# The first MLP's gate computed beside its up product, and the rest of layer 0's conditioning in steps of 512 columns

## The chip, the core and the metric

The kernel runs on one core of one Trainium2 chip. A core has TensorE (PE; its weight loads are listed apart as PEld), VectorE (DVE), ScalarE (ACT), GpSimd (POOL) and SyncE (SP, which here issues most transfers), each with a queue of its own that it works through in order; they meet only at semaphores. The metric is the device time of one execution in microseconds.

## The reference, cut to what matters

The program is one inference step of a two-layer trunk for a prompt of 1024 tokens and a sample of 32 tokens, so 1056 token columns in all. Every layer is conditioned: from a vector `c` (one for the prompt, one for the sample) six vectors of 1024 values come out of one matrix, and scale, shift and gate the two sublayers.

```python
def ada_mod(c, w, b):
    return jax.nn.silu(c) @ w + b
...
for l in range(DEPTH):
    sh1, sc1, g1, sh2, sc2, g2 = jnp.split(ada_mod(c, p['w_ada'][l], p['b_ada'][l])[:, None, :], 6, axis=-1)
    u = x * (1 + sc1) + sh1
    if l < N_A_LAYERS:
        y, cv, C, n, m = mlstm_mixer(u, ...)
    else:
        ... # attention on one shared K/V, itself conditioned by w_ada_kv
    x = layer_norm(ALPHA * x + (1 + g1) * y, p['ln_g'][l, 0], p['ln_b'][l, 0])
    u = x * (1 + sc2) + sh2
    f = jnp.square(jax.nn.relu(u @ p['w_up'][l])) @ p['w_down'][l]
    x = layer_norm(ALPHA * x + (1 + g2) * f, p['ln_g'][l, 1], p['ln_b'][l, 1])
```

All is in 32-bit floats. `g2` of layer 0, the first MLP's gate, is the one that the change moves. `g1`, `sh2` and `sc2` of layer 0 are what else is computed beside the mLSTM; `sh1` and `sc1` come before it.

## The kernel before

**Matmuls.** Activations lie with features on the partitions and tokens along the row. To keep 32-bit accuracy at the fast matmul rate, `split` writes a high half of a tile (a cast on ScalarE, L89) and the remainder (a subtraction on VectorE, L90); `proj` (L118 to L120) then multiplies high by high, high by low and low by high. Weights come in blocks of 512 rows by 256 columns through a ring of three `raw` buffers and are split into a ring of six `wc` buffers.

**Stages of layer 0.** The start loads and transposes the input. The mLSTM projects `v`, `q`, `k` and the output gate `o` head by head and runs the matrix memory chunk by chunk between those matmuls. The output projection (`op_a`) and the first norm follow. Then the MLP, `mlp7`: some blocks of the up projection are computed plainly (`up_tile`), the others in the class `Seven` by seven products instead of eight per 2 x 2 block, whose weight forms (`rdn_u` to `s_u` to `wf_u`) VectorE and ScalarE make one job ahead. Activations are squared, split (`HL`, one buffer) and stored to memory (`hpl`). The down projection of layer 0 (`dn_plain`) goes over eight groups of 512 rows: per group eight feature chunks by token blocks (264 columns in the first group, else 384 or 288), twelve matmuls a tile, and an eviction on VectorE that multiplies by the gate and adds to `ACX` (L1045). The tile takes one of the eight PSUM banks until then. In group 0, four weight blocks `w_dn_0_0` to `w_dn_0_3` serve four tiles by two chunks each, that is eight tiles each.

**Conditioning.** A product of a vector with a matrix is done on VectorE: `cs` holds silu(c) with one value per partition, and a multiply-add takes a slice of the matrix (128 rows by some columns), multiplies by that value and adds to an accumulator, for each of the two vectors and eight slices of 128 rows. `ada_cols` (L238, L241) does this in steps of 256 columns (two chunks of 128), `ada_wide` (L274, L276) in steps of 512 with the next load under way. A transpose (L245, L283) and a sum (L246, L285) put partial sums into `cx`, and every eight chunks `ada_sums` finishes with four small matmuls (`adas`, L296) and an addition into `ada`.

**Order.** Python generators are woven by `Flow`. A generator yields how long it wants to wait; every unit of matmul work calls `flow.tick(us)`, which counts the waits down and runs a generator one step when its wait is used up. `flow.finish(gen)` runs a generator to its end at once. A scheduler then sets the static order of each engine's queue with the order of emission as priority; within `Seven`, TensorE's order is that of emission. Three generators carry the conditioning: `ada_l0` beside the mLSTM (32 chunks for layer 0 from column 2048, in a `wc` buffer of its own called `ada_room`, waits `ADA_C`), `ada_some` in `Seven` (8 chunks for the shared K/V, waits `ADA_B = (4.0, 2.0, 1.0, 8.0)`, accumulator `aacc` and loads `rada` in the `raw` ring), and `ada_rest` in the down projection (56 chunks, accumulator `aw`, loads `radw`). The tick of a product of `Seven` is `QN / L.pace`, that is 264 / 480 = 0.55 in layer 0, and there are 154 products. Between the two MLP halves stands:

```python
def seven():
    norms["ada"] = flow.add(ada_some())

def down():
    flow.finish(norms["ada"])
    norms["ada"] = flow.add(ada_rest(), carry=True)
```

## Time and profile before

| | us |
|---|---|
| median of 3 runs | 2436.86 |
| lowest and highest | 2434.49, 2437.28 |
| the profiled execution | 2437.59 |
| its span | 2435.8 |
| VectorE busy in the span | 1987.5 |
| ScalarE busy | 1178.8 |
| first and last conditioning multiply-add beside the mLSTM, start | 70.7, 447.6 |
| the same in `Seven` (`aacc`) | 640.3, 776.7 |
| the same in the down projection (`aw`) | 869.8, 1165.5 |

A row of the profile names a line of the program, an engine, an operation, and what it writes and reads (buffer numbers left out). A wait row says who waited, for whom, the total, how often and the longest. In a time-ordered list a row has its start, the time from the first start to the last end of what it merges, how many (`x8`), and in brackets the idle time ahead of it with what ended it. Durations of instructions in a row overlap at their ends, so the spacing is a little under the duration. Tables of stretches give the busy time of each engine between two points of the span.

### The profile page before, as it was taken

How to read it: one execution, taken by the hardware profiler on the slowest of the kernel's cores; microseconds unless marked ns; L12 is line 12 of the kernel's file. 1: busy time of each engine (PE TensorE's matmuls, PEld its weight loads, DVE VectorE, ACT ScalarE, POOL GpSimd, SP SyncE). 2: the span in 40 equal slices, each digit the busy share in tenths (PEclk: the TensorE clock that was granted, in tenths of full speed). 3: DMA queues.
4: the chain of work that ended last, by engine and by line, in shares of the span. 5: the costliest groups of instructions: out<-in, count | busy, mean ns of one | idle time of the engine just before them, and what ended most of it. 6: DMA issues, size and time to landing. Idle time of an engine off the chain costs nothing.

```text
span 2435.8 us, 44452 instructions
## 1 busy us (share of the span) xinstructions
PE 2363.6 (97%) x17180; PEld 2265.8 (93%) x17180; DVE 1987.5 (82%) x4222; ACT 1178.8 (48%) x2394; POOL 166.6 (7%) x315
## 2 busy tenths in 40 slices
PE   7999999999999999999999999999999999899997
PEld 4999999999999999999989977889999999899997
DVE  4899898788788789999697666755998888887778
ACT  4644456278566620010157566763776777222212
POOL 0211100000000000000001134420000000000003
PEclk9999999999999999999999999999999999999999
DMA  8433223436556897656423220051486779966642
GB/s 297 128 103 98 82 86 102 158 113 215 182 186 194 296 343 266 234 203 232 143 64 97 74 64 1 11 133 36 162 279 233 252 255 341 367 242 232 229 151 72
DMA packets 292151, 423.61 MB, mean 174 GB/s; under 512 B 15576, under 2 KB 221804, under 8 KB 286820
## 3 DMA queue, kind: packets, MB, share of 16 engines
q1 hardware_dynamic: 287908, 390.50, 48.3%
q10 hardware_dynamic: 4032, 30.28, 3.1%
q8 instruction: 135, 2.21, 0.4%
q14 instruction: 76, 0.62, 0.1%
HBM read 304.91 MB, written 118.17 MB: 174 GB/s over the span
## 4 chain that ended last, share of the span: by engine, by line
PE 47%; DVE 12%; DMA 5%; ACT 4%; issue 2%; POOL 1%; SPq 0%; DVEq 0%; ACTq 0%; POOLq 0%
PE dn L1415 11%; PE up L1280 9%; PE dn L120 5%; PE dn L119 5%; PE dn L118 5%; PE pv L1853 3%; PE s L1796 2%; PE pt L1831 2%; DMA rdn_u<-in_w_up_dram 1%; DVE wf_u L90 1%; PE op_b L118 1%; PE op_b L119 1%; PE op_b L120 1%; DVE HL L90 1%; DMA radw<-in_w_ada_dram 1%
## 5 line engine op out<-in xcount | busy, mean ns | idle before, releaser
L1045 DVE SCALAR_TENSOR_TENSOR ACX<-dn,ada,ACX 128x264 f32<-128x264 f32 (+6 forms) x664 | 281.9, 448 | 86.4 <-PE dn L1415 41.4
L1415 PE MATMUL dn<-fx,wf_d 128*128 128x264 f32 x2016 | 254.0, 285 | 6.5 <-DVE ACX L1045 3.5
L1415 PEld LDWEIGHTS dn<-fx,wf_d 128*128 128x128 f32 x2016 | 248.7, 188 | 8.7 <-issue 2.5
L89 ACT CAST w_dn<-raw_dn 128x1024 fp32r<-128x1024 f32 x36 | 37.7, 1050 | 284.1 <-DVE aw L274 172.8
L118 PE MATMUL dn<-hs,w_dn 128*128 128x384 f32 (+2 forms) x512 | 161.3, 316 | 0.8 <-DVE ACX L1045 0.7
L119 PE MATMUL dn<-hs,w_dn 128*128 128x384 f32 (+2 forms) x512 | 160.9, 315 | 0.0
L120 PE MATMUL dn<-hs,w_dn 128*128 128x384 f32 (+2 forms) x512 | 155.9, 314 | 1.8 <-DVE w_dn L90 1.8
L1280 PE MATMUL up<-TF,wf_u 128*128 128x264 f32 x1056 | 143.6, 285 | 1.8 <-ACT H L1283 1.8
L1280 PE MATMUL up<-u,wf_u 128*128 128x264 f32 x1056 | 139.7, 285 | 1.7 <-DVE H L1286 0.8
L1280 PE MATMUL up<-U,wf_u 128*128 128x264 f32 x1056 | 139.6, 285 | 1.6 <-DVE H L1286 1.0
L274 DVE SCALAR_TENSOR_TENSOR aw<-radw,cs,aw 128x512 f32<-128x512 f32 x196 | 139.5, 745 | 0.0
L1280 PEld LDWEIGHTS up<-TF,wf_u 128*128 128x128 f32 x1056 | 134.3, 188 | 3.1 <-ACT H L1283 3.0
L1280 PEld LDWEIGHTS up<-U,wf_u 128*128 128x128 f32 x1056 | 133.1, 188 | 2.7 <-DVE H L1286 1.9
L1280 PEld LDWEIGHTS up<-u,wf_u 128*128 128x128 f32 x1056 | 132.6, 188 | 2.7 <-ACT wf_u L89 0.8
L119 PE MATMUL dn<-U,w_dn 128*128 128x384 f32 (+2 forms) x416 | 129.8, 313 | 0.0
L118 PE MATMUL dn<-U,w_dn 128*128 128x384 f32 (+2 forms) x416 | 129.3, 311 | 0.0
L120 PE MATMUL dn<-U,w_dn 128*128 128x384 f32 (+2 forms) x416 | 125.6, 312 | 0.9 <-DVE w_dn L90 0.9
L238 DVE SCALAR_TENSOR_TENSOR ada_room<-ada_room,cs 128x256 f32<-128x256 f32 x224 | 98.9, 476 | 4.2 <-DMA ada_room<-in_w_ada_dram 4.2
L120 PEld LDWEIGHTS dn<-hs,w_dn 128*128 128x128 f32 x512 | 95.8, 188 | 2.9 <-DVE w_dn L90 2.6
L118 PEld LDWEIGHTS dn<-hs,w_dn 128*128 128x128 f32 x512 | 96.4, 188 | 1.5 <-DVE ACX L1045 1.0
L119 PEld LDWEIGHTS dn<-hs,w_dn 128*128 128x128 f32 x512 | 96.5, 188 | 0.0
L1806 DVE CUSTOM_DVE_ANT_0 p<-s,bias 128x576 f32<-128x576 f32 (+9 forms) x132 | 79.1, 606 | 20.3 <-PE s L1796 13.4
(394 smaller groups left out, 7171.5 us busy)
## 6 DMA issues: line engine op xcount, KB each, us to landing
hpl<-HL SPq DMA_DIRECT2D x144, 264.0 KB
rdn_u<-in_w_up_dram SPq DMA_DIRECT2D x64, 512.0 KB
hd<-HL SPq DMA_DIRECT2D x28, 1056.0 KB
fx<-hd SPq DMA_DIRECT2D x50, 528.0 KB
radw<-in_w_ada_dram SPq DMA_DIRECT2D x24, 1024.0 KB
hd<-HM SPq DMA_DIRECT2D x28, 792.0 KB
raw_up<-in_w_up_dram SPq DMA_DIRECT2D x40, 512.0 KB
raw_dn<-in_w_down_dram SPq DMA_DIRECT2D x36, 512.0 KB
```

The costliest lines, as they stand in the source:

```text
L90: (eng or nc.vector).tensor_sub(dst_l, src, dst_h.bitcast(F32))
L118: nc.tensor.matmul(ps, wh, mov(0, k), start=(k == 0), stop=False)
L119: nc.tensor.matmul(ps, wh, mov(1, k), start=False, stop=False)
L120: nc.tensor.matmul(ps, wl, mov(0, k), start=False, stop=(k == nk - 1))
L238: nc.vector.scalar_tensor_tensor(acc[:, cnd], raw[:, k], sc, acc[:, cnd], op0=ALU.mult, op1=ALU.add)
L274: nc.vector.scalar_tensor_tensor(acc[cnd], raw[:, k], sc, acc[cnd], op0=ALU.mult, op1=ALU.add)
L1045: nc.vector.scalar_tensor_tensor(xs, ps[:, off + o:off + o + mm_], gate[:, fc, cnd:cnd + 1], xs, op0=ALU.mult, op1=ALU.add)
L1280: nc.tensor.matmul(p, self.ws[w][:, wl, k], moving(f, tp, xl, k), start=first and k + n_ == 0, stop=k == 3 and n_ == 2, skip_group_check=n ...
L1415: nc.tensor.matmul(p, ws[w][:, wl, k], t[:, s0, xl], start=first and k + n_ == 0, stop=k == kg - 1 and n_ == 2, skip_group_check=not first)
L1796: nc.tensor.matmul(s[:, b, :w], qst, kk[i][:, g, k0 + j0:k0 + j0 + w], start=(i == 0), stop=(i == 1))
L1806: nc.vector.tensor_tensor_reduce(out=z.rearrange("p (b w) -> p b w", b=np_), in0=s[:, :np_, :w], in1=bt.rearrange("p (b w) -> p b w", b=np ...
L1853: nc.tensor.matmul(pv[64 * e:64 * e + 64, :nq], V[:kp, vt0 + j, g * 64:(g + 1) * 64], pts[e][:kp, j, :nq], start=(j == 0), stop=(j == nt - 1))
```

## The change

The generator beside the mLSTM drops the eight chunks of the first MLP's gate (part 5 of layer 0, from column 5 x 1024) and does the other 24 by `ada_wide` in steps of 512 columns. Its loads are of 1 MB, into the first 2048 columns of `ada_room`, which the two transposes use afterwards; there is no second room, so a new argument `ahead=False` loads a step's matrix when the step begins, waits 3.0, does half the work, waits 2.0 and does the rest. The accumulators are a tile of the `raw` ring, `ada_acc`, held from the first step to the last. The eight chunks go to the head of `ada_some`, in steps of 256 columns as its own, with a finish of the gate (`ada_fix`) between the two sets of eight.

```diff
-    def ada_wide(src, c0, base, nch, mk, tmp_f, raw_f, step):
+    def ada_wide(src, c0, base, nch, mk, tmp_f, raw_f, step, ahead=True):
...
-        load(0)
-        yield step[0]
+        if ahead:
+            load(0)
+            yield step[0]
         for i, (j, half) in enumerate(jobs):
-            load(i + 1)
+            load(i + ahead)
+            if not ahead:
+                yield step[1]
...
-                if k % 2:
+                if k % 2 and (ahead or k == 1):
                     yield step[k // 2]
...
-    ADA_C = (2.0, 0.0, 2.0)
+    ADA_C = (2.0, 3.0, 2.0)
...
     def ada_l0():
         room = ring.tile([P, 2112], F32, tag="wc", name="ada_room", bufs=6)
 
+        acc = raw_tile([P, 2, 512], "ada_acc")
+
         def raw_f(shape, name):
-            return room[:, 1024:2048].rearrange("p (k c) -> p k c", k=4)
+            return room[:, :2048].rearrange("p (k c) -> p k c", k=4)
 
         def tmp_f(shape, name):
-            return room[:, 512:1024] if len(shape) == 2 else room[:, :512].rearrange("p (k c) -> p k c", k=2)
-        yield from ada_cols(a["w_ada"][0], 2048, 16, 32, adat, tmp_f, ADA_C, raw_f)
-        ada_fix(0, [(2, "g"), (4, "sc"), (5, "g")])
+            i = int(name[-1])
+            return room[:, 512 * i:512 * i + 512] if name.startswith("awt") else acc[:, i]
+        yield from ada_wide(a["w_ada"][0], 2048, 16, 24, adat, tmp_f, raw_f, ADA_C, False)
+        ada_fix(0, [(2, "g"), (4, "sc")])
...
     def ada_some():
+        yield from ada_cols(a["w_ada"][0], 5 * D, 40, 8, mm, tmp_t, ADA_B)
+        ada_fix(0, [(5, "g")])
         yield from ada_cols(a["w_ada_kv"], 0, 96, 8, mm, tmp_t, ADA_B)
```

**VectorE's queue at the start of the down projection.** `H` and `HL` are the last activations of the up projection, `ACX` the evictions of the first `dn` tiles, `aw` the conditioning of `ada_rest`, `w_dn` the remainder halves of down weights. Before:

```order
L90 TENSOR_TENSOR HL_15_1_10324<-H_15_1_10098,HL_15_1_10324 128x4x264
L1286 TENSOR_TENSOR H_13_1_10232<-up_13_1_2_10331,H_13_1_10232 128x264
L1045 SCALAR_TENSOR_TENSOR ACX_0_10118<-dn_0_0_0_10408,ada,ACX_0_10118 128x264
L1045 SCALAR_TENSOR_TENSOR ACX_0_10118<-dn_0_0_264_10424,ada,ACX_0_10118 128x264
L276 TENSOR_SCALAR aw_0_0_10469<-radw_0_0_10422,cs 128x512
L276 TENSOR_SCALAR aw_0_1_10470<-radw_0_0_10422,cs 128x512
L1045 SCALAR_TENSOR_TENSOR ACX_0_10118<-dn_0_0_528_10438,ada,ACX_0_10118 128x264
L274 SCALAR_TENSOR_TENSOR aw_0_0_10469<-radw_0_0_10422,cs,aw_0_0_10469 128x512
L274 SCALAR_TENSOR_TENSOR aw_0_1_10470<-radw_0_0_10422,cs,aw_0_1_10470 128x512
L1045 SCALAR_TENSOR_TENSOR ACX_0_10118<-dn_0_0_792_10452,ada,ACX_0_10118 128x232
```

Now (`aacc` is the accumulator of `ada_some`, `aat` its transpose):

```order
L90 TENSOR_TENSOR HL_15_1_10158<-H_15_1_9918,HL_15_1_10158 128x4x264
L1292 TENSOR_TENSOR H_13_1_10066<-up_13_1_2_10165,H_13_1_10066 128x264
L1051 SCALAR_TENSOR_TENSOR ACX_0_9942<-dn_0_0_0_10317,ada,ACX_0_9942 128x264
L90 TENSOR_TENSOR w_dn_0_1_10181<-raw_dn_0_1_10179,w_dn_0_1_10181 128x1024
L238 SCALAR_TENSOR_TENSOR aacc_2_10058<-rada_2_1_10246,cs,aacc_2_10058 128x256 x8
L1051 SCALAR_TENSOR_TENSOR ACX_0_9942<-dn_0_0_264_10333,ada,ACX_0_9942 128x264
L90 TENSOR_TENSOR HL_13_1_10230<-H_13_1_10066,HL_13_1_10230 128x4x264
L245 STREAM_TRANSPOSE aat_2_10256<-aacc_2_10058 128x512
L241 TENSOR_SCALAR aacc_4_10259<-rada_4_0_10260,cs 128x256
L246 TENSOR_REDUCE cx<-aat_2_10256 128x16
L241 TENSOR_SCALAR aacc_4_10259<-rada_4_0_10260,cs 128x256
L238 SCALAR_TENSOR_TENSOR aacc_4_10259<-rada_4_0_10260,cs,aacc_4_10259 128x256 x6
```

Before, four evictions stand among the first four `aw` operations. Now the rest of `ada_some` stands there: 36 multiply-adds, 4 scalings, 3 transposes and 3 sums follow the first eviction, with the second, third and fourth eviction at wide gaps among them. The remainder half of the third weight block, `w_dn_0_2`, comes after the eviction of the thirteenth tile before, and of the sixteenth now, each time ahead of the seventeenth, its first user.

**SP's queue at the same place.** `raw_dn` are down weights on their way in, `radw` the loads of `ada_rest`, `hpl` the stores of activations. Before:

```order
L96 DMA raw_dn_0_0_10274<-in_w_down_dram 128x4x256
L96 DMA raw_dn_0_1_10345<-in_w_down_dram 128x4x256
L1147 DMA hpl_6125<-HL_12_1_10206 256x1x264 x4
L96 DMA raw_dn_0_2_10663<-in_w_down_dram 128x4x256
L96 DMA raw_dn_0_3_10802<-in_w_down_dram 128x4x256
L1624 DMA ACX_1_10406<-xsp_80 128x2112
L261 DMA radw_0_0_10422<-in_w_ada_dram 128x4x512
L1147 DMA hpl_6125<-HL_15_1_10324 256x1x264 x4
L261 DMA radw_0_1_10467<-in_w_ada_dram 128x4x512
L1624 DMA ACX_1_10406<-xsp_80 128x2112
L1147 DMA hpl_6125<-HL_13_1_10392 256x1x264 x4
L261 DMA radw_4_0_10567<-in_w_ada_dram 128x4x512
```

Now (`rada` are the loads of `ada_some`):

```order
L231 DMA rada_2_1_10246<-in_w_ada_kv_dram 128x4x256
L1153 DMA hpl_5931<-HL_15_1_10158 256x1x264 x4
L231 DMA rada_4_0_10260<-in_w_ada_kv_dram 128x4x256
L231 DMA rada_4_1_10270<-in_w_ada_kv_dram 128x4x256
L231 DMA rada_6_0_10284<-in_w_ada_kv_dram 128x4x256
L1153 DMA hpl_5931<-HL_13_1_10230 256x1x264 x4
L261 DMA radw_0_0_10331<-in_w_ada_dram 128x4x512
L231 DMA rada_6_1_10294<-in_w_ada_kv_dram 128x4x256
L261 DMA radw_0_1_10376<-in_w_ada_dram 128x4x512
L1632 DMA ACX_1_10315<-xsp_80 128x2112
L261 DMA radw_4_0_10476<-in_w_ada_dram 128x4x512
L96 DMA raw_dn_0_2_10572<-in_w_down_dram 128x4x256
```

Five of the sixteen loads of `ada_some` now stand between the down weights and the stores, a sixth just ahead of the first `raw_dn`, and the third and fourth down weights have moved behind them and behind three loads of `ada_rest`.

**TensorE's queue, eleventh tile of the down projection.** Before, the tile's matmuls follow each other:

```order
L118 MATMUL dn_0_2_528_10573<-U,w_dn_0_1_10347 128x264
L119 MATMUL dn_0_2_528_10573<-U,w_dn_0_1_10347 128x264
L120 MATMUL dn_0_2_528_10573<-U,w_dn_0_1_10347 128x264
L118 MATMUL dn_0_2_792_10587<-U,w_dn_0_1_10347 128x264
L119 MATMUL dn_0_2_792_10587<-U,w_dn_0_1_10347 128x264
L120 MATMUL dn_0_2_792_10587<-U,w_dn_0_1_10347 128x264
```

Now the four small matmuls that end the second set of `ada_some` stand in it:

```order
L120 MATMUL dn_0_2_528_10482<-U,w_dn_0_1_10181 128x264
L118 MATMUL dn_0_2_792_10496<-U,w_dn_0_1_10181 128x264
L119 MATMUL dn_0_2_792_10496<-U,w_dn_0_1_10181 128x264
L299 MATMUL adas_6_10307<-cx,sel 32x16 x4
L120 MATMUL dn_0_2_792_10496<-U,w_dn_0_1_10181 128x264
L118 MATMUL dn_0_2_792_10496<-U,w_dn_0_1_10181 128x264
L118 MATMUL dn_0_1_792_10430<-U,w_dn_0_0_10110 128x264
```

They read `cx`, so everything behind them in TensorE's queue waits for the last sum on VectorE. The eighth tile (`dn_0_1_792`) is also put behind the ones of the next chunk.

## The prediction

> **What bounds the kernel.** I read the page first (busy time and the chain that ended last), then the table of stretches, then the waits of TensorE, then the tiles of the conditioning work, and last the time-ordered list around the place where layer 0 turns from its up to its down projection.
>
> ```profile
> PE 2363.6 (97%) x17180; PEld 2265.8 (93%) x17180; DVE 1987.5 (82%) x4222; ACT 1178.8 (48%) x2394; POOL 166.6 (7%) x315
> ```
>
> TensorE is busy 97% of the span, so time moves only where TensorE starts or stops waiting. The table of stretches has, behind each stretch's length, the busy time (and instructions) of PE, PEld, DVE, ACT and POOL, then granted clock, DMA share and GB/s:
>
> ```profile
> 61.00:122.00 61.00, 58.67 (x373) 57.30 (x372) 53.57 (x96) 36.97 (x78) 12.69 (x20) 0.97 0.43 128
> 120.00:426.00 306.00, 303.52 (x2017) 286.07 (x2016) 281.56 (x858) 162.66 (x439) 29.18 (x94) 1.00 0.31 94
> 606.00:806.00 200.00, 197.21 (x1606) 195.66 (x1606) 157.55 (x276) 121.31 (x214) 0.00 (x0) 1.00 0.62 197
> 740.00:760.00 20.00, 19.09 (x155) 18.71 (x155) 18.94 (x37) 13.58 (x24) 0.00 (x0) 1.00 0.59 186
> 806.00:862.00 56.00, 54.92 (x453) 54.18 (x452) 43.90 (x72) 40.00 (x70) 0.00 (x0) 1.00 0.89 295
> 868.00:890.00 22.00, 22.00 (x183) 22.00 (x182) 21.34 (x41) 3.08 (x3) 0.00 (x0) 1.00 1.04 383
> 862.00:1160.00 298.00, 296.53 (x1957) 292.77 (x1956) 283.49 (x509) 30.04 (x30) 0.00 (x0) 1.00 0.70 255
> ```
>
> The mLSTM (about 61 to 426) leaves TensorE idle 2.3 + 2.5 us in all, though VectorE is 92% busy. The seven-product up projection (606 to 862) leaves 3.9 us. The down projection (from 862) is the tight one: VectorE 95% busy beside a TensorE that hardly waits, with the DMA engines full at its start. So what leaves the mLSTM leaves a place where it cost little, and what arrives at 806 to 890 arrives where there is least room.
>
> **What the mLSTM loses.** Conditioning there before (count, then min/median/max ns), and, in the time-ordered list, such instructions when they stand in a row:
>
> ```profile
> L238 DVE SCALAR_TENSOR_TENSOR ada_room<-ada_room,cs x224: 451/476/696, 70.7 to 447.6; 128x256 f32<-128x256 f32 x112
> L241 DVE TENSOR_SCALAR ada_room<-ada_room,cs x32: 308/345/355, 70.1 to 437.6; 128x256 f32<-128x256 f32 x32
> L245 DVE STREAM_TRANSPOSE ada_room<-ada_room x16: 679/700/712, 83.3 to 449.2; 128x512 f32<-128x512 f32 x16
> ```
> ```profile
> 773.93 3.25 DVE L238 SCALAR_TENSOR_TENSOR aacc<-rada,cs,aacc 128x256 f32<-128x256 f32 x8
> 868.56 0.88 DVE L276 TENSOR_SCALAR aw<-radw,cs 128x512 f32<-128x512 f32 x2 [1.59 <-DMA radw<-in_w_ada_dram]
> 886.53 1.29 DVE L283 STREAM_TRANSPOSE awt<-aw 128x512 f32<-128x512 f32 x2
> 924.68 2.74 DVE L274 SCALAR_TENSOR_TENSOR aw<-radw,cs,aw 128x512 f32<-128x512 f32 x4
> ```
>
> Eight multiply-adds of 256 columns take 3.25 us, so one costs 0.40; four of 512 take 2.74, so 0.67. Before: 224 x 0.40 + 32 x 0.31 + 16 transposes and 16 sums at 0.64 = 120 us. After: six groups of 512 columns, 84 x 0.67 + 12 x 0.42 + 12 x 2 x 0.64 = 77 us. VectorE is relieved of about 43 us. TensorE can get back only what it waits:
>
> ```profile
> PE ae_ps L567 <- ACT stk L560: 2.2, 1, 2.2
> PE cu L678 <- DVE hn L704: 2.0, 5, 0.9
> ```
>
> The second wait is VectorE's lateness; the first is the gate rows' chain, which VectorE also feeds. I take **-2 us**. Bounds: -4.8 (all idle time of both stretches) to +5.3. The latter is for the new accumulator, which holds one of three raw buffers through the stage, and for the 1 MB loads that wait in SP's queue ahead of weights: one weight load that comes a whole landing late, 5.32 us by the load quoted next. I stay near the first end because the weights' loads stand tiles ahead of use. The conditioning's last sums come earlier, so the first output gate isn't late.
>
> ```profile
> 729.18 5.32 DMA rdn_u<-in_w_up_dram
> ```
>
> **What the up projection gains.** `ada_some` now has eight jobs of two chunks, not four. A product ticks 264/480 = 0.55. The waits 4, 2, 4, 2, 1 then take 8, 4, 8, 4, 2 = 26 ticks a job, and 15 instead of 2 where a set of eight chunks ends. The first set ends at tick 118, as before. 22 jobs of weights x 7 products give 154 ticks, so the second set is only 36 ticks in when the stage ends: one job and the first four operations of the next are done there, and the rest is drained at once by the call at the start of the down projection.
>
> In the 36 products (36 x 12 matmuls x 0.12 us = 52 us, so 811 to 862) VectorE gets 20 x 0.40 + 4 x 0.31 + 1.3 = 10.5 us, where it had 12.1 us idle. The nearest row is 740:760, where such work ran before: VectorE 95% busy and 155 matmuls in 20 us, against 20/0.12 = 166, 7% lost; 806:862 has 453 of 466, 3% lost. 4% more of 52 us is 2. These jobs also take a raw buffer and a temporary that the weight forms use, and the last five weight jobs are single ones, so forms are due twice as often: **+3 us**, between 0 and 10.5 (all on the path).
>
> **What the down projection's start gains.** The time-ordered list of before, VectorE, then ScalarE, then TensorE:
>
> ```profile
> 861.26 1.26 DVE L90 TENSOR_TENSOR HL<-H,HL 128x1056 fp32r<-128x1056 f32 x1 [0.54 <-ACT HL L89]
> 862.43 0.43 DVE L1286 TENSOR_TENSOR H<-up,H 128x264 f32<-128x264 f32 x1
> 865.02 0.49 DVE L1045 SCALAR_TENSOR_TENSOR ACX<-dn,ada,ACX 128x264 f32<-128x264 f32 x1 [2.16 <-PE dn L120]
> 866.48 0.49 DVE L1045 SCALAR_TENSOR_TENSOR ACX<-dn,ada,ACX 128x264 f32<-128x264 f32 x1 [0.96 <-PE dn L120]
> ...
> 871.08 0.61 DVE L1045 SCALAR_TENSOR_TENSOR ACX<-dn,ada,ACX 128x232 f32<-128x232 f32 x2
> 871.61 0.74 DVE L274 SCALAR_TENSOR_TENSOR aw<-radw,cs,aw 128x512 f32<-128x512 f32 x1
> ...
> 874.50 0.88 DVE L1045 SCALAR_TENSOR_TENSOR ACX<-dn,ada,ACX 128x264 f32<-128x264 f32 x2
> ...
> 884.59 1.21 DVE L90 TENSOR_TENSOR w_dn<-raw_dn,w_dn 128x1024 fp32r<-128x1024 f32 x1
> ```
> ```profile
> 871.91 1.08 ACT L89 CAST HL<-H 128x1056 fp32r<-128x1056 f32 x1 [6.75 <-DMA hpl<-HL]
> ```
> ```profile
> 863.37 0.28 PE L118 MATMUL dn<-U,w_dn 128*128 128x264 f32 x1
> ```
>
> The first `dn` tile starts at 863.37; twelve matmuls at 0.12 make 1.45 us a tile, so the seventeenth tile, the first to need the third weight block, starts near 886.5. That block's VectorE half is done at 885.8: it has under 1 us to spare. Let zero be the first eviction (865.02); the seventeenth tile then is at 21.5.
>
> In the new order VectorE has, from that eviction to the end of the same weight block: 36 multiply-adds (14.4), 4 scalings (1.2) and 3 transposes and 3 sums (3.8), which is the drained conditioning, 19.4 us; sixteen tiles' evictions (twelve whole blocks at 0.40, since two take 0.88 and one 0.49, and four in two pieces at 0.53, from 871.08 to 871.61: 6.9); 14 multiply-adds and two scalings of the next layer's conditioning (10.2); one HL difference and two weight halves (1.2 + 2 x 1.15). Sum 40 us. All of it stands ahead of the third block's end, so the tile can't start before: 40 - 21.5 = 18.5.
>
> To this come waits in VectorE's own queue. The last HL cast waits for the store of the HL before it: 871.91, 9.4 us after that one's difference ended (862.5). In the new order VectorE reaches the last HL 5 us after the first eviction, and the cast can end no sooner than about 9: 4 us, and nothing behind it may pass. The drained loads go through the same three raw buffers while the DMA share is 1.04; most have been under way for over 5.3 us when they are due. The third block's own load now stands in SP's queue behind them and 4 MB of others, 4 MB / 383 GB/s = 11 us from 18 us on, still before VectorE is free for it. Sum **+22 us**. Bounds: 10 (if the 4.7 us that VectorE idles there before, and TensorE's eight PSUM banks, 8 x 1.45 us, each cover part of it), and 33 (two 512 KB loads each a landing late).
>
> TensorE's queue also has the last sums' matmuls in the middle of the eleventh tile, waiting for the last reduction, 28 us in; so TensorE stands still for some 10 us there. What that does to its clock:
>
> ```profile
> 1245.00:1255.00 10.00, 8.55 (x51) 7.86 (x50) 9.91 (x14) 5.36 (x8) 0.00 (x0) 1.00 0.32 88
> 1255.00:1265.00 10.00, 6.46 (x33) 5.48 (x32) 9.88 (x16) 4.91 (x9) 0.00 (x0) 0.93 0.40 122
> 1265.00:1275.00 10.00, 9.97 (x43) 10.00 (x44) 7.82 (x15) 3.48 (x7) 0.00 (x0) 0.73 0.01 2
> ```
>
> Around 1260 TensorE idled 5 us and the granted clock fell to 0.93 and 0.73 in the next two rows: (0.07 + 0.27) x 10 = 3.4 us lost. Here the slow tiles would run while VectorE is still the later one, so I take **+1**, between 0 and 3.4. The Trainium skill (page "TensorE: Matmul & The Clock Gate", section "What's actually happening") says that after an idle window of some 3.4 us the array runs at half rate until it has been busy that long; the trace agrees (3.4 us lost). By that rule alone the term would be 3.4 a pause and the sum 2.4 us higher.
>
> From the seventeenth tile on the queues stand as before, so nothing is given back: the down projection is TensorE's and nobody there waits for conditioning that ends later. Of the loads, 32 of 512 KB in the mLSTM become 12 of 1 MB there and 8 of 512 KB in the up projection: the same bytes, but 2.6 MB of them now fall into the full stretch.
>
> **Sum.** -2 + 3 + 22 + 1 = +24 us. The profiled execution took 2437.59 us, 0.7 above the median of 2436.86; on the median this gives **2461 us**.
>
> **Rivals.** (1) The drain is mostly covered: PSUM run-ahead and VectorE's idle time take half, term 10, Seven +1, mLSTM -2: 2446. For it: 4.7 us idle at 862 to 872. Against: the third block stands behind all of it in VectorE's queue, and has no 1 us to spare. Chance 0.15. (2) The drain waits for memory: 2.6 MB more at 383 GB/s is 7 us, and one or two late landings: 2471 to 2478. For it: DMA share 1.04. Chance 0.12. (3) Faster: the drain is covered altogether. VectorE's idle 12.1 us before 862 and 4.7 after, with eight banks' 11.6, are 28 us against 30 us that arrive; the mLSTM then gives its 4.8: 2433. It decides at the third block: if that is late by less than 4 us, faster wins. Against: that block has under 1 us. Chance 0.05, and 0.03 that gain and loss cancel within 0.2%. (4) The mLSTM holds more than idle time shows: its weight loads are busy 286 of 306 us, so relief could win up to 19.9 us: 2461 - 18 = 2443. Against: its matmuls follow each other at the rate of the later stretches,
>
> ```profile
> 206.10 0.28 PE L480 MATMUL v<-w_v,U 128*128 128x256 f32 x1
> 206.22 0.28 PE L481 MATMUL v<-w_v,U 128*128 128x256 f32 x1
> 206.33 0.28 PE L479 MATMUL v<-w_v,U 128*128 128x256 f32 x1
> ```
>
> 0.12 apart; chance 0.03. The Trainium skill (page "Perfetto Trace Analysis", section "Identifying the Most-Contended Engine") says to judge TensorE's headroom by the busy share of weight loads, not of matmuls: by that rule this rival would hold.
>
> **Chances.** The likeliest case, 0.62, lies in 2453 to 2470. The range takes in (1) and most of (2): 2445 to 2473. 0.2% is 4.9 us, about what a measurement here can tell from no change. Slower 0.92, same 0.03, faster 0.05.
>
> **What would show it.** Right: VectorE's busy share in 120 to 426 down from 92% to under 82% with TensorE's hardly moved; an unbroken run of `aacc` multiply-adds behind the first `dn` eviction; TensorE waiting 10 us or more for `adas`, and then for `w_dn`; a granted clock under 1 there. Wrong: `w_dn` on time at the seventeenth tile, or the mLSTM's end earlier by over 5 us.

## The result, and the profile after

The changed kernel takes 2476.55 us (median of five runs, 2474.87 to 2482.26), the kernel before on the same chip 2437.28 us. The ratio is 1.0166, with a 95% interval of 1.0155 to 1.0177: 39 us slower, where 24 were forecast, and outside the range given (2445 to 2473). The profiled execution took 2482.26 us, the slowest of the five, so the terms that its trace gives add up to 44 us and not to 39.

The page of the changed kernel, busy times. The matrix products are the same in number, VectorE does a little less than before, and the span is 44.6 us longer:

```profile
PE 2375.2 (96%) x17180; PEld 2276.6 (92%) x17180; DVE 1980.1 (80%) x4126; ACT 1181.2 (48%) x2394; POOL 164.9 (7%) x315
```

To find where the time went, I set the start of each matrix product of the changed kernel against the start of the same product before (the k-th product of a tile against the k-th of that tile). The lag is -0.3 us at 800 us (by the clock of before), 12.2 in the down projection's third `dn` tile, 46.8 once the third weight block is in use (920 to 940), 44.1 from 1300 on. So the loss is in two neighbouring places: 12.5 us in the late up projection and 34.6 at the down projection's start; 2.7 come back later. The first `dn` tile can't be the border between the two. Its lag is only 9.3, but it now runs ahead of the up projection's last 24 products, which stood ahead of it before:

```profile
872.63 0.28 PE L118 MATMUL dn<-U,w_dn 128*128 128x264 f32 x1
...
874.32 3.07 PE L1286 MATMUL up<-U,wf_u 128*128 128x264 f32 x24
877.23 0.28 PE L118 MATMUL dn<-U,w_dn 128*128 128x264 f32 x1
```

The table of stretches, of the changed kernel (columns as in the prediction):

```profile
120.00:426.00 306.00, 303.81 (x2019) 286.53 (x2018) 260.47 (x740) 165.56 (x445) 28.60 (x95) 1.00 0.30 91
806.00:862.00 56.00, 46.95 (x366) 45.20 (x366) 40.02 (x74) 32.07 (x57) 0.00 (x0) 0.97 0.79 260
872.00:890.00 18.00, 16.77 (x139) 16.57 (x137) 15.21 (x30) 7.18 (x10) 0.00 (x0) 1.00 0.97 304
890.00:911.00 21.00, 3.01 (x12) 2.70 (x12) 7.96 (x20) 0.00 (x0) 0.00 (x0) 0.65 1.03 389
911.00:921.00 10.00, 5.86 (x34) 5.62 (x35) 9.76 (x23) 1.05 (x1) 0.00 (x0) 0.53 0.88 293
```

In the mLSTM (first row) VectorE's share fell from 92% to 85%, and TensorE gained 0.3 us. At the down projection's start (rows from 872) VectorE is not full throughout, against the forecast: between 890 and 911 it was busy 8 of 21 us and TensorE 3, while the DMA share stood at 1.03. For most of that stretch both waited, in the end for one load. VectorE's queue of the changed kernel, in order of time, from the drained conditioning on:

```profile
880.92 3.25 DVE L238 SCALAR_TENSOR_TENSOR aacc<-rada,cs,aacc 128x256 f32<-128x256 f32 x8
884.09 0.49 DVE L1051 SCALAR_TENSOR_TENSOR ACX<-dn,ada,ACX 128x264 f32<-128x264 f32 x1
...
887.47 5.62 DVE L238 SCALAR_TENSOR_TENSOR aacc<-rada,cs,aacc 128x256 f32<-128x256 f32 x14
893.02 0.48 DVE L1051 SCALAR_TENSOR_TENSOR ACX<-dn,ada,ACX 128x264 f32<-128x264 f32 x1
...
895.13 2.46 DVE L238 SCALAR_TENSOR_TENSOR aacc<-rada,cs,aacc 128x256 f32<-128x256 f32 x6
910.62 3.25 DVE L238 SCALAR_TENSOR_TENSOR aacc<-rada,cs,aacc 128x256 f32<-128x256 f32 x8 [13.04 <-DMA rada<-in_w_ada_kv_dram]
913.79 0.45 DVE L1051 SCALAR_TENSOR_TENSOR ACX<-dn,ada,ACX 128x232 f32<-128x232 f32 x1
```

The run of `aacc` multiply-adds is there, with evictions (`ACX`) far apart in it, and it is broken by 13.04 us in which VectorE waited for the drain's last load. The chain that ended last has that load, with its time from issue to landing, behind the multiply-adds that read its buffer before it (they end at 889.95):

```profile
889.45 0.50 DVE aacc L238 x2
889.96 20.57 DMA rada<-in_w_ada_kv_dram
910.62 3.25 DVE aacc L238 x8
```

So it was issued when a raw buffer came free. SyncE's queue shows what it then stood behind: four `hpl` stores and a load of 1 MB.

```profile
876.28 3.00 SPq L1153 DMA_DIRECT2D hpl<-HL  x4
879.33 5.24 SPq L231 DMA_DIRECT2D rada<-in_w_ada_kv_dram  x3
885.87 2.84 SPq L1153 DMA_DIRECT2D hpl<-HL  x4
888.75 0.83 SPq L261 DMA_DIRECT2D radw<-in_w_ada_dram  x1
889.96 3.92 SPq L231 DMA_DIRECT2D rada<-in_w_ada_kv_dram  x1
```

Issued at 889.96 (the issuing alone took SyncE 3.92 us), it took 20.57 us where I had reckoned with 5.3. VectorE was free for it at 897.6, so after 5.3 us it would have been in time. The drain's loads that were issued from 863.8 to 884.2 did land as reckoned, after 4.7 to 6.7 us, at a DMA share that was already 0.97 (row from 872). These times are read from the trace's semaphore updates, of which a transfer makes sixteen, by its last one. Of the last load's sixteen, fifteen came within 10.8 us and one after 20.57; why that one came so late stays open.

And TensorE's queue in the same place, its first products after each of two pauses, then its waits for `dn` tiles from 606 to 1160:

```profile
893.55 0.59 PE L118 MATMUL dn<-U,w_dn 128*128 128x264 f32 x1 [4.78 <-DVE ACX L1051]
893.94 0.42 PE L119 MATMUL dn<-U,w_dn 128*128 128x264 f32 x1
894.16 0.42 PE L120 MATMUL dn<-U,w_dn 128*128 128x264 f32 x1
...
915.14 0.56 PE L118 MATMUL dn<-U,w_dn 128*128 128x264 f32 x1 [18.58 <-DVE ACX L1051]
```
```profile
PE dn L118 <- DVE ACX L1051: 25.9, 3, 18.6
```

TensorE ran through its PSUM banks (nine tiles) and then waited 4.8 us, 18.6 us and, at 930.8, 2.5 us for an eviction (`ACX`) that stood behind other work in VectorE's queue, the first two behind the drained work. It did not wait for `adas`, and 0.3 us for a weight block, the two that I had named.

In the up projection, the waits of TensorE between 806 and 863:

```profile
PE up L1286 <- ACT wf_u L89: 6.7, 2, 3.4
PE up L1286 <- DVE H L1292: 1.5, 1, 1.5
PE up L1286 <- ACT H L1289: 0.8, 2, 0.6
```

Weight forms came late twice, 3.4 us each. The chain that ended last has, before the second, a `rdn_u` load that went out the moment the paced job's multiply-adds (`aacc`) were through with a raw buffer:

```profile
856.79 0.48 DVE aacc L238
857.29 3.87 DMA rdn_u<-in_w_up_dram
861.19 0.69 DVE s_u L1250
```

The last multiply-add ended at 857.27. The weights thus waited for a buffer that conditioning held. For the first late form this is not shown: its load went out at 828.61, half a microsecond after the last reader of a paced load (828.1), but SyncE was busy with other transfers until 828.2.

The waits in this stretch are 9.0 us, 1.1 in the kernel before. Most of what is missing to 12.5 is TensorE's clock. Behind each of the two long waits products stand 0.22 us apart instead of 0.12 for 3.3 and 4.0 us, and in all such spacing costs 4.4 us more than before; the granted clock is 0.97 in the row from 806.

### The profile page after: what moved, and what is told of

It reads as the page before. It is cut to its first block, busy times and chain, and to the rows that moved or that the text cites. A ratio compares the mean times of both kernels' runs of the same rounds, so it can differ in the third digit from the quotient of the medians.

```text
span 2480.4 us, 44339 instructions
## 1 busy us (share of the span) xinstructions
PE 2375.2 (96%) x17180; PEld 2276.6 (92%) x17180; DVE 1980.1 (80%) x4126; ACT 1181.2 (48%) x2394; POOL 164.9 (7%) x315
## 4 chain that ended last, share of the span: by engine, by line
PE 47%; DVE 13%; DMA 4%; ACT 3%; issue 2%; SPq 1%; POOL 0%; DVEq 0%; ACTq 0%; POOLq 0%
PE dn L1421 11%; PE up L1286 8%; PE dn L120 5%; PE dn L119 4%; PE dn L118 4%; PE pv L1861 3%; PE s L1804 2%; PE pt L1839 2%; DMA rdn_u<-in_w_up_dram 1%; DVE wf_u L90 1%; DMA rada<-in_w_ada_kv_dram 1%; DVE HL L90 1%; PE q L120 1%; PE q L119 1%; PE q L118 1%
## 5 line engine op out<-in xcount | busy, mean ns | idle before, releaser
L118 PE MATMUL dn<-U,w_dn 128*128 128x384 f32 (+2 forms) x416 | 131.6, 319 | 25.9 <-DVE ACX L1051 25.9
L118 PEld LDWEIGHTS dn<-U,w_dn 128*128 128x128 f32 x416 | 80.9, 195 | 26.7 <-issue 18.9
L90 DVE TENSOR_TENSOR HL<-H,HL 128x1056 fp32r<-128x1056 f32 x64 | 80.2, 1253 | 19.8 <-ACT HL L89 19.8
```

The costliest lines, as they stand in the source:

```text
L90: (eng or nc.vector).tensor_sub(dst_l, src, dst_h.bitcast(F32))
L118: nc.tensor.matmul(ps, wh, mov(0, k), start=(k == 0), stop=False)
```

## The experiments

Each kernel ran beside the kernel before. The lag at six places, found as above, in each kernel's profiled execution (us; the places by the clock of before), and the ratio of the timed runs. The column at 867 is the third `dn` tile, by which all of the up projection is done; the expectations were written with the border at the first tile, hence their 9.5 and 37 us.

| kernel | 400 | 800 | third `dn`, 867 | 930 | 1180 | 1340 | ratio (95%) |
|---|---|---|---|---|---|---|---|
| changed | 0.1 | -0.3 | 12.2 | 46.8 | 46.5 | 44.1 | 1.0166 (1.0155 to 1.0177) |
| e1_wide | 1.5 | 0.1 | 1.6 | 1.0 | 1.0 | 0.9 | 1.0002 (0.9993 to 1.0011) |
| e2_move | 2.8 | 2.6 | 15.5 | 46.0 | 45.6 | 42.4 | 1.0152 (1.0136 to 1.0168) |
| e3_kv_late | -1.7 | -2.6 | 0.9 | 0.4 | 0.3 | 30.3 | 1.0127 (1.0113 to 1.0141) |
| e4_no_drain | -1.9 | -2.6 | 12.5 | 19.8 | 16.5 | 44.3 | 1.0175 (1.0160 to 1.0191) |
| e5_dve_burst | 0.4 | 1.3 | 2.9 | 19.3 | 19.0 | 16.6 | 1.0054 (1.0037 to 1.0070) |
| e6_dma_burst | 0.2 | 0.6 | 1.9 | 17.3 | 14.5 | 13.7 | 1.0058 (1.0045 to 1.0072) |
| e7_short_hold | 0.5 | 2.2 | 7.8 | 26.2 | 25.9 | 23.4 | 1.0098 (1.0083 to 1.0114) |
| e8_all_in_up | 0.3 | 13.1 | 24.6 | 25.5 | 25.2 | 22.7 | 1.0087 (1.0071 to 1.0102) |
| e9_wc | -1.6 | -1.4 | 4.4 | 25.5 | 25.2 | 21.6 | 1.0099 (1.0083 to 1.0116) |
| e10_kv_late_quick | 1.0 | 1.3 | 2.5 | 10.5 | 22.1 | 19.9 | 1.0075 (1.0062 to 1.0088) |
| e12_burst_no_loads | -1.9 | -1.1 | 10.4 | 31.7 | 31.5 | 29.0 | 1.0108 (1.0093 to 1.0123) |
| e13_no_kv_loads | -0.2 | -1.8 | 1.2 | 17.0 | 16.7 | 13.2 | 1.0052 (1.0037 to 1.0067) |
| e14_kv_early | 0.3 | 30.2 | 29.0 | 28.5 | 28.4 | 26.5 | 1.0120 (1.0103 to 1.0137) |
| e15_kv_early_quick | 6.5 | 22.9 | 21.9 | 22.7 | 22.5 | 20.6 | 1.0088 (1.0073 to 1.0103) |
| e16_rest_later | -0.7 | -0.3 | 10.9 | 31.3 | 27.9 | 38.6 | 1.0178 (1.0160 to 1.0196) |

A lag of one to three microseconds at 400 and 800 says nothing here: kernels that are alike up to there differ by as much (the changed kernel and e3_kv_late at 800: -0.3 and -2.6). Each lag is from one execution, and these lie from 4.6 us below (e7_short_hold) to 7.1 us above (e2_move) their kernel's median, the changed kernel's 5.7 above: a difference between two rows that is no larger than that shows nothing.

### The two halves of the change

The first kernel keeps the gate in the mLSTM and takes only the wide steps (the diff is against the changed kernel).

```diff
-        yield from ada_wide(a["w_ada"][0], 2048, 16, 24, adat, tmp_f, raw_f, ADA_C, False)
-        ada_fix(0, [(2, "g"), (4, "sc")])
+        yield from ada_wide(a["w_ada"][0], 2048, 16, 32, adat, tmp_f, raw_f, ADA_C, False)
+        ada_fix(0, [(2, "g"), (4, "sc"), (5, "g")])
...
     def ada_some():
-        yield from ada_cols(a["w_ada"][0], 5 * D, 40, 8, mm, tmp_t, ADA_B)
-        ada_fix(0, [(5, "g")])
```

> All 32 chunks of layer 0 in the mLSTM in steps of 512 columns, nothing moved into the up projection. Theory (the whole loss is made by the gate's arrival in the up projection): 2435 to 2438, as before or up to 2 us faster, since the changed kernel's trace gains 0.5 us by 800 us. Rival (the 1 MB loads and the accumulator in a third raw buffer cost something that shows only later, in the state that the mLSTM leaves): 2442 or more.

Measured: 2438.63 us, no difference. Its trace, in the mLSTM:

```profile
120.00:426.00 306.00, 304.01 (x2019) 286.01 (x2018) 271.81 (x760) 163.59 (x443) 28.39 (x95) 1.00 0.31 95
```

VectorE did 10 us less in this stretch, weight loads were busy as long as before (286.0 against 286.1 us) and TensorE won 0.5. Relief of VectorE there is worth nothing, and the fourth rival, that it would win some of the weight loads' idle 20 us, is refuted. The rule of the Trainium skill (page "Perfetto Trace Analysis", section "Identifying the Most-Contended Engine") that the prediction set beside it, to judge TensorE's headroom by the busy share of its weight loads, says how much room there is and not that relief of another engine opens it; here that relief opened none.

The second moves the gate alone (against the kernel before):

```diff
-        yield from ada_cols(a["w_ada"][0], 2048, 16, 32, adat, tmp_f, ADA_C, raw_f)
-        ada_fix(0, [(2, "g"), (4, "sc"), (5, "g")])
+        yield from ada_cols(a["w_ada"][0], 2048, 16, 24, adat, tmp_f, ADA_C, raw_f)
+        ada_fix(0, [(2, "g"), (4, "sc")])
...
     def ada_some():
+        yield from ada_cols(a["w_ada"][0], 5 * D, 40, 8, mm, tmp_t, ADA_B)
+        ada_fix(0, [(5, "g")])
```

> The gate alone moved, the 24 chunks left in the mLSTM in steps of 256 columns as before. Theory: 2474 to 2479, all of the change's loss. Rival (the wide form in the mLSTM pays for part of the loss, as forecast at 2 us): 2478 to 2480.

Measured: 2473.82 us; its ratio agrees with the changed kernel's within the intervals. The whole loss is the gate's arrival in the up projection.

### What the drain is made of

A burst of VectorE work without loads, and loads with next to no work, each put into the kernel before, in `L0.down()` behind `flow.finish(norms["ada"])`, where the drain stands. First the burst: five halves of eight operations as in `ada_cols`, all on one buffer that is set to zero first (0.91 us more), three transposes and sums, four small matmuls on `cx` and a copy of their result.

```diff
+            raw = raw_tile([P, 4, 256], "burst")
+            nc.vector.memset(raw, 0.0)
+            for j in range(3):
+                acc_ = tmp_t([P, 2, 256], f"bacc{j}")
...
+            nc.vector.tensor_copy(tmp_t([P, 16], "bout"), ps[:, :16])
```

Then the loads:

```diff
+            for j in range(5):
+                raw = raw_tile([P, 4, 256], f"burst{j}")
+                nc.sync.dma_start(raw, a["w_ada_kv"][512 * (j % 2):512 * (j % 2) + 512, 256 * j:256 * j + 256].rearrange(
+                    "(k p) c -> p k c", p=P))
+                nc.vector.tensor_scalar(tmp_t([P, 16], f"bt{j}"), raw[:, 0, :16], cs[:, 0, 0:1], None, op0=ALU.mult)
```

> The kernel before, with a burst of VectorE work where the drain stands in the changed kernel: 40 operations of 128x256, three transposes and three sums on one buffer that is already there, and the four small matmuls that wait for the last sum; no loads, and its results are used by nothing. Theory (VectorE's queue alone, as forecast): 2456 to 2461. Rival (the drain waits for its loads; VectorE's time is mostly covered by the eight PSUM banks and its idle time): 2442 to 2450, and then the rest of the 37 us that the drain costs in the changed kernel's trace belongs to the loads.

Measured: 2450.9 us, between the two expectations. In its trace the lag grows from 2.9 to 19.3 us at the drain, 16.4 (the medians are 13.3 us apart), and TensorE waits for evictions as in the changed kernel, but less long:

```profile
PE dn L118 <- DVE ACX L1045: 9.9, 2, 7.9
```

> The kernel before, with five loads of 512 KB into the raw buffers at the same place, each read by one operation of 128x16. Theory (loads cost only where much work waits for them, here next to none): 2437 to 2444. Rival (memory is the bound there, so 2.6 MB more cost their 7 us and push the weights back): 2445 to 2455.

Measured: 2451.79 us. My theory was wrong and the rival right: five loads with no work cost 15.4 us at that place (lag 1.9 to 17.3; about 5 come back by 1500). TensorE's waits between 820 and 930, and the chain that ended last:

```profile
PE dn L118 <- ACT w_dn L89: 13.8, 1, 13.8
```
```profile
874.30 11.72 DMA hpl<-HL
886.04 15.24 DMA raw_dn<-in_w_down_dram
```

A store of 264 KB needed 11.7 us, and the third weight block, issued only when that had landed, another 15.2. In the trace the two transfers tell their landing on the same semaphore, one of eight, and the load's only wait is for it. Burst and loads come to 16.4 + 15.4 = 32 us, near the 34.6. By itself that proves little: here TensorE waited for the third weight block, in the changed kernel for evictions behind the drain's last load.

The next two kernels take loads away from the changed kernel and leave the work in place; the diff is of e12_burst_no_loads in `ada_cols`, and e13_no_kv_loads has the condition without `j >= 4`.

```diff
-                raw = raw_f([P, 4, 256], f"rada_{base}_{j}_{half}")
+                none = base == 96 and j >= 4
+                if not none:
+                    raw = raw_f([P, 4, 256], f"rada_{base}_{j}_{half}")
...
+                        x = ident[:, None, :].broadcast_to([P, 2, P]) if none else two(raw[:, k])
```

> As changed, but the last two of the second set's four jobs (those that are wholly drained) read no loads: the same operations of the same size on a constant that is already there, so their part of the conditioning is wrong; four loads of 512 KB fewer. Theory (the start's 37 us are VectorE's burst, some 16 to 20, and the loads, some 15 to 17): 2458 to 2464. Rival (VectorE's burst alone): 2472 to 2478.

Measured: 2465.59 us, a little above the theory's range. The start costs 21.3 us (10.4 to 31.7) and the up projection 11.5, near the changed kernel's 12.5.

> As changed, but the whole second set reads the constant: none of its eight loads and none of its raw buffers, the same VectorE work at the same places; that part of the conditioning is wrong. Theory (the up projection's 9 us are weights that wait for raw buffers and for memory): against the run without the last four loads another 5 to 8 us less, 2450 to 2457. Rival (they are VectorE's time): as that run, 2458 to 2464.

Measured: 2451.38 us, as the theory had it. The start costs 15.8 us, as in e5_dve_burst, and the up projection 3.0 instead of 12.5. The multiply-adds take as long as before (478 and 479 ns in the median, on loads and on the constant). So VectorE's work is 3 us of the up projection's loss and 16 of the start's, and the rest of both goes with the loads and the buffers that they take.

### Buffers or memory

> As changed, with other pauses in the two-chunk jobs: a load is used five ticks after its issue and not twelve, and the job pauses after its sum instead, so that it holds a raw buffer less than half as long; the first set ends at about tick 113 and the drain is nearly as long. Theory (the up projection's 9.5 us are weight loads that wait for a raw buffer which a paced job holds): they fall under 4, in all 2467 to 2473. Rival (they are VectorE's and memory's volume): 2474 to 2479.

```diff
-    ADA_B = (4.0, 2.0, 1.0, 8.0)
+    ADA_B = (2.0, 0.5, 8.0, 15.0)
```

Measured: 2461.09 us, 15 us better than the changed kernel and more than either side expected. The up projection lost 5.6 us after 800 (7.3 with what was lost ahead of that), so the theory holds only in part there; but the start cost 18.4 where the same burst was expected. The next kernel gives the loads other buffers:

```diff
-        yield from ada_cols(a["w_ada_kv"], 0, 96, 8, mm, tmp_t, ADA_B)
+        yield from ada_cols(a["w_ada_kv"], 0, 96, 8, mm, tmp_t, ADA_B, wc_tile)
```

> As changed, but the second set's loads take buffers of the ring of six (weight forms, wide conditioning) and not of the three raw ones. Theory (late loads at the start because a raw buffer must come free first, and weights in the up projection that wait for a raw buffer): both terms shrink, 2455 to 2466. Rival (memory alone is late, whatever the buffer): 2472 to 2480. Against the theory works that the forms then lack a buffer of six.

Measured: 2460.97 us, as the theory had it: 5.8 us in the up projection, 21.1 at the start. What the two have in common is in the rows on the loads of the second set: their issues from first to last, and for how long VectorE waited for them. The changed kernel, e7_short_hold and e9_wc:

```profile
L231 SPq DMA_DIRECT2D rada<-in_w_ada_kv_dram x8: 368/374/3922, 814.9 to 890.0; - x8
its engine sat idle before it (us, times) until:
  DMA rada<-in_w_ada_kv_dram: 15.2, 3
```
```profile
L231 SPq DMA_DIRECT2D rada<-in_w_ada_kv_dram x8: 368/376/694, 796.8 to 877.9; - x8
its engine sat idle before it (us, times) until:
  DMA rada<-in_w_ada_kv_dram: 1.8, 2
```
```profile
L231 SPq DMA_DIRECT2D rada<-in_w_ada_kv_dram x8: 367/578/1147, 814.4 to 876.7; - x8
its engine sat idle before it (us, times) until:
  DMA rada<-in_w_ada_kv_dram: 6.4, 2
```

The same eight loads, the last issued 12 to 13 us earlier, and the start costs 13 to 16 us less (by the medians both kernels are 15.5 us faster in all). With more buffers, or buffers that are held for less long, the last load went out ahead of the four stores and the load of 1 MB, and by its semaphore updates it landed after 5.3 us (e7_short_hold) and 6.2 us (e9_wc). The Trainium skill (page "Perfetto Trace Analysis", section "Optimization Strategy") says that the same gap, repeating on an engine that should be full, can mean too little room for the next tile. Here it was a single gap of 13 us, and the buffers are all that the source of e9_wc changes.

The other side, that loads of 1 MB crowd out the last one:

```diff
-            norms["ada"] = flow.add(ada_rest(), carry=True)
+            norms["ada"] = flow.add(ada_rest(), 20.0, carry=True)
```

> As changed, but layer 1's conditioning starts 20 ticks later, so that its first loads of 1 MB are issued behind the drain's last load and behind the first late weights. Theory (the drain's last load lands after 20.6 us because 1 MB loads and others share the memory with it): 2466 to 2473. Rival (it is late because it is issued late, its buffer coming free at 889 us, and the loads of 1 MB do not matter): 2474 to 2479.

Measured: 2478.31 us, which reads like the rival, but the trace says otherwise. The last load was issued at 889.7 as in the changed kernel, VectorE waited 7.9 us for it and not 13.0, and the start cost 20.4 us instead of 34.6. Of these 14 us, 10.7 were lost again at 1230 to 1300 (lag 27.9 to 38.6), where the conditioning that had been put off is due; the medians show no gain. The load landed after 14.3 us by its semaphore updates, against 20.6. So both count: the late buffer and what else is under way in memory.

### Can the work go elsewhere?

> As changed, but the call that drains the second set at the down projection's start is taken out: its rest goes on a few operations a tile and layer 1's conditioning follows it. The up projection is as in the changed kernel. Theory: the 9.5 us that the up projection lost stay and the 37 us at the start go: 2446 to 2452. Rival (volume): 2465 or more. If also the up projection's 9.5 us go: 2437 to 2441.

```diff
         def down():
-            flow.finish(norms["ada"])
-            norms["ada"] = flow.add(ada_rest(), carry=True)
+            norms["some"] = norms["ada"]
...
+                yield from norms["some"]
+                yield from ada_rest()
```

Measured: 2481.13 us. The start's cost fell to 7.3 us, but the conditioning then was not finished at the first block's end, and another 28 us were lost at 1230 to 1300. The up projection's loss stayed (a lag of 12.5 at its end, 12.2 in the changed kernel).

> As changed, but the second set (eight chunks of the third block) is not in the up projection: it is computed with its other half in the paced work behind the drain, in steps of 512 columns. Nothing is drained and the up projection holds eight chunks, as before. Theory (the burst and the raw buffers in the late up projection are the loss): 2436 to 2446; some 26 us of multiply-adds more for VectorE in a down projection where it is 95% busy, but none of them waited for. Rival (VectorE's volume in the down projection is the loss, burst or not): 2455 to 2465.

```diff
     def ada_some():
         yield from ada_cols(a["w_ada"][0], 5 * D, 40, 8, mm, tmp_t, ADA_B)
         ada_fix(0, [(5, "g")])
-        yield from ada_cols(a["w_ada_kv"], 0, 96, 8, mm, tmp_t, ADA_B)
...
-        yield from ada_wide(a["w_ada_kv"], D, 104, 8, mm, tmp_t, wc_tile, ADA_W)
+        yield from ada_wide(a["w_ada_kv"], 0, 96, 16, mm, tmp_t, wc_tile, ADA_W)
```

Measured: 2467.92 us; missed. Up to 1200 us it stands as the kernel before (lag 0.3), so neither the late up projection nor the start loses anything without the second set there. Then 30 us go at 1230 to 1300, where TensorE waits for the norm:

```profile
PE var_n L929 <- ACT qr_n L89: 13.2, 2, 12.2
PE mean_n L929 <- ACT sr_n L89: 5.6, 2, 3.2
PE q L118 <- ACT w_q L89: 5.1, 1, 5.1
```

Its conditioning ends at 1217 where that of the kernel before ends at 1177, and the norm's first sum starts at 1217.9 where it started at 1213.6. Some of the 30 us are the clock, 0.84 in 1200 to 1320 against 0.97 before; how 4 us of delay become 30 I did not follow further. The next kernel lets the same work end in time:

```diff
-    ADA_W = (4.5, 4.5, 2.0)
+    ADA_W = (4.0, 4.0, 2.0)
```

> As the run with the second set in the later, paced work, but with pauses of 4.0 instead of 4.5 there, so that 16 groups of loads take 292 of the 319 ticks before the first block's end and nothing is left to drain there. Theory (that run's 30 us came all from such a drain at the end, since its trace has +0.3 us until 1200): 2434 to 2440. Rival (VectorE, at 95% in the down projection, has no room for 26 us more): 2450 to 2465.

Measured: 2457.12 us; the rival was right. Nothing is lost at the norm, but the lag grows evenly from 2.5 at 880 to 22.1 at 1180. The stretch from 880 to 1200, before and in this kernel:

```profile
880.00:1200.00 320.00, 318.25 (x2057) 313.89 (x2056) 295.01 (x551) 31.03 (x30) 0.00 (x0) 1.00 0.64 232
```
```profile
880.00:1200.00 320.00, 304.59 (x1945) 296.67 (x1944) 308.76 (x549) 27.89 (x27) 0.00 (x0) 0.99 0.65 234
```

VectorE goes from 295 to 309 busy of 320 us and TensorE does 112 products less in that time. TensorE's waits there are for weight halves that VectorE makes (`w_dn`, 12.2 us in 15 waits). The run before, with its longer pauses, had VectorE busy 309.35 us in the same stretch and lost nothing up to 1200. So some 14 us more fit into the down projection beside TensorE; the 26 us of this kernel did not, and cost 20.

> As changed, with shorter pauses in the two-chunk jobs (2.0, 1.5, 1.0, 3.0), so that all eight jobs end at about tick 136 of 154 and nothing is drained. Theory: the start's 37 us go, the up projection loses 8 to 16 us since its jobs stand closer: 2445 to 2455. Rival (the late up projection is at its limit, each of 16 chunks more costs its whole 2.4 us of VectorE and more in weights): 2460 or more.

```diff
-    ADA_B = (4.0, 2.0, 1.0, 8.0)
+    ADA_B = (2.0, 1.5, 1.0, 3.0)
```

Measured: 2459.82 us. There is no drain and the start loses 0.9 us, but the up projection loses 24.6, of them 13 ahead of 800 us: closer jobs cost there too, more than the 8 to 16 expected.

Last, the wide steps make room in the mLSTM, so the second set was put there as well (against e1_wide, without the second set in the up projection), first at the pace of the changed kernel and then faster, as the last two lines have it.

```diff
         ada_fix(0, [(2, "g"), (4, "sc"), (5, "g")])
+        yield from ada_wide(a["w_ada_kv"], 0, 96, 8, adat, tmp_f, raw_f, ADA_C, False)
...
-    ADA_C = (2.0, 3.0, 2.0)
+    ADA_C = (1.5, 2.0, 1.0)
```

> All 32 chunks of layer 0 and the second set's eight in the mLSTM, in steps of 512 columns; no conditioning at all in the up projection and nothing to drain. Theory (VectorE's time in the mLSTM costs nothing up to where it was, 120 us before and some 115 now; the up projection gives back its 3 to 4 us of waits): 2433 to 2438. Rival (the mLSTM has no room for it, the gate rows wait): 2440 to 2450.

Measured: 2467.36 us; both expectations missed. Up to 425 us nothing is lost (0.3); then the rest is drained at the mLSTM's end and 35 us go between 425 and 600.

> As the run with all conditioning of the two sets in the mLSTM, with shorter pauses there (1.5, 2.0, 1.0), so that ten groups of two loads take some 80 ticks where the eight of the run with wide steps alone took 96, and nothing is drained at the mLSTM's end. Theory (that run's 29 us came from a drain at the mLSTM's end, the third place where one costs that much): 2432 to 2440. Rival (VectorE's volume in the mLSTM): 2445 to 2465.

Measured: 2458.95 us; missed, the rival's size. Its waits between 50 and 610:

```profile
PE op_a L118 <- ACT w_oa L89: 10.6, 1, 10.6
PE op_a L120 <- DVE w_oa L90: 5.3, 1, 5.3
```

The faster pace costs 6.5 us in the mLSTM, and at its end the output projection's weights (`w_oa`) come late; the last two groups are still at work there (VectorE's multiply-adds run until 466). It was not ended in time, so whether the second set would be free in the mLSTM stays open. No version here is faster than the kernel before.

## Why the prediction was right or wrong

**Right: the direction, and the two places.** The loss is where the moved work arrives, and e2_move shows that it is all of it.

**The mLSTM, -2 us.** The trace gives -0.3 at 800 us, and e1_wide no difference. The reason held: VectorE's relief is worth at most TensorE's waits. VectorE's share fell to 85%, not to the 82% that I had named.

**The start, +22 us: this is the step that failed.** It was 34.6. VectorE's own queue was 18.5 in the sum and measured 16.4 (e5_dve_burst) and 15.8 (e13_no_kv_loads). That this is so near is in part luck: I had counted the 18.5 us up to the third weight block, and TensorE stood still at PSUM banks whose evictions were queued behind the burst, ahead of `adas` and `w_dn`. The 4 us for the last `HL` were not there: its row at 884.58 has no wait, since VectorE came to it late enough (e5_dve_burst has 2.35). What was wrong is that waiting for the drained loads was put at nothing, since most "have been under way for over 5.3 us when they are due". The last one had been, for 7.6 us: it was issued at 889.96, when a raw buffer came free, and VectorE came to it at 897.6. But it took 20.6 us and not 5.3, and VectorE waited 13. The 5.3 came from a row at 729. It held for the drained loads that were issued up to 884, and for the last one too where that was issued ahead of the stores and the load of 1 MB (e7_short_hold, e9_wc); it did not hold behind them. I had written 4 MB at 383 GB/s for the weights behind these loads, and nothing of the kind for the loads themselves. The trace of before had such landings as well: two loads of 512 KB, issued at 881.05 and 885.83 behind loads of 1 MB, landed after 14.2 and 13.5 us by their semaphore updates, and TensorE hardly waited for the block (0.3 us). Without the second set's loads the start costs 15.8 us, so they are 19 of the 34.6. The upper bound of 33, two landings of 5.3 each, was too low for the same reason.

**The up projection, +3 us.** It was 12.5, above its upper bound of 10.5. VectorE's share of it was sized rightly: e13_no_kv_loads loses 3.0. The other 9.5 go with the loads and their buffers. I had written a sentence on the raw buffers and given it no number of its own; held for a shorter time or taken from the other ring, the stage loses 5.6 (e7_short_hold) and 5.8 us (e9_wc), so the buffers are some 7 of them.

**The clock, +1 us.** It cost some 11 us, which lie inside the two terms above. Behind each of TensorE's five pauses of 2.5 us or more products stood 0.22 us apart instead of 0.12: for 3.3 and 4.0 us in the up projection, and for 2.6, 5.3 and 6.7 us at the start, after pauses of 4.8, 18.6 and 2.5 us; after one of 1.6 us it was a single product. That is 4.4 us of the up projection's 12.5 and 6.7 of the start's 34.6; the granted clock was 0.53 in the row from 911. I had reckoned with one pause, and with none in the up projection. The Trainium skill's rule (page "TensorE: Matmul & The Clock Gate", section "What's actually happening") speaks of half rate after an idle window of some 3.4 us, until as long has been busy; here a pause of 2.5 us was enough, and three of the five slow stretches lasted longer. The 3.4 us a pause that I had worked out from it is also wrong by itself: half rate for 3.4 us loses half of them.

**Nothing given back later.** 2.7 us came back.

**The rivals.** The second, that the drain waits for memory (2471 to 2478), gives the measured time, and its mechanism is what the runs show, beside VectorE's and not in its place. I gave it 0.12. That its time fits is in part luck: it priced memory at 10 to 17 us, where the loads cost 19 at the start, and it had the up projection at +3. What misled me is that in the kernel before nothing waits there at the same DMA share: its loads are issued ahead of need, and the drain's last one was not issued far enough ahead. The first and third fell with e5_dve_burst: a burst is not half covered there, it costs 16 of its 20 us by itself, 13 by the medians.

## What to carry to other kernels

A burst of work on an engine's queue cost most of its length here (16 of 20 us), and its loads cost as much again, because the last one got its buffer late and went out behind stores and larger loads: ask of every load not only when it is needed but what must end before it can be issued, and what is issued just ahead of it. Take landing times from loads that stand behind the same traffic as the one in question; the DMA share alone does not tell. Count the products at a lower clock behind every pause. Work that is moved off a busy engine gains only what was waited for there, and must end before the next deadline: wherever conditioning ran up to one (the start at 863, the norm at 1230, the mLSTM's end at 425), 28 to 35 us went.

## What the runs showed of the hardware

A load of 512 KB that landed after 4.7 to 6.7 us when it was issued from 863.8 to 884.2 in the changed kernel (DMA share 0.97 in the row from 872) took 20.6 us when it was issued at 889.96, right behind four stores of 264 KB and a load of 1 MB (share 1.03); in e6_dma_burst one took 15.2 and a store of 264 KB 11.7. So a share near 1 does not say how long a transfer takes. The Trainium skill (page "DMA: Bandwidth & Descriptors", section "Latency and other measured facts") gives the latency of memory under high load as 2 us; that is not the landing time of a whole transfer behind others, which is what was measured here. Five such loads with almost no work behind them cost the kernel as much (ratio 1.0058) as 40 VectorE operations, three transposes and three sums without loads (1.0054).
